# Latent columns ahead of the banded attention's in the input projection, normalising after the values, and another order at the start of the feed-forward stage

## The chip, the cores and the metric

The kernel runs on one core of a Trainium2 chip. The time is device microseconds of one launch: the median of three runs was 1651.15 us before the change (1648.31 to 1651.73). A profile was taken of one more execution. The engines are TensorE (PE in the rows, PEld its weight loads), VectorE (DVE), ScalarE (ACT), GpSimd (POOL) and SyncE (SP, which here only starts transfers). Each takes its instructions in a fixed order and waits at the first whose inputs or places are not ready.

## What is computed

One layer of a hybrid model, for a prompt of 128 tokens and a latent grid of 1024. Each is modulated, goes through one input projection, then through three kinds of heads, an output projection and a gated feed-forward part:

```
z = h @ w_in                       # 1024 -> 256 + 128 + 32 | 256 + 128 + 128 | 512
o_mla = softmax(q k^T) v           # latent attention, 8 heads, 1024 + 256 keys
o_swa = softmax(band, context, sink) v     # banded attention, 4 heads
cu = conv_module(u)                # 31 taps over 256 channels
x = x + g1 * (concat(o_mla, o_swa, cu) @ w_out)
x = x + g2 * ((silu(dwconv(h @ w_up)[gate]) * dwconv(h @ w_up)[value]) @ w_down)
```

The first 416 columns of `z` (cq, ckv, kr) belong to the latent attention, the next 512 to the banded one, the last 512 to the convolution.

## The kernel before

There are nine tiles of 128 tokens: tile 0 is the prompt, 1 to 8 the grid. Every float32 product is three matrix products (`mm3`, lines 61 to 63): an operand is split into a rounded high part and the rest, and high by high, high by low and low by high are added up in one bank. So whatever becomes an operand is split first: a copy or cast to the high part on ScalarE, and a subtraction on VectorE (lines 69, 72, 77) or, after a plain copy, two operations on GpSimd (`split_turned`, lines 607 to 609: copy `pf` on ScalarE, `ph` and `pl` on GpSimd).

A scheduler with a model of each engine's times orders the instructions of every engine when the program is built; the order in the source and the tiles' buffers bound it. The stages by the trace:

- To 75 us: loads and modulation. To 126: the convolution's columns (`convolved`). VectorE then works at the taps of the convolution (line 552, 128x1167 each), which fill it until 200 us.
- 126 to 183: the banded attention's 512 columns, for tiles 0 to 4 and then 5 to 8, a tile's product being 24 matmuls. `later_half` calls between them make the modulation's later pieces; their weights are loaded into the places of `cqH` and `cqL`, which are free until the latent columns come. Each tile is rotated on VectorE (lines 434, 439, 440) into `zs`.
- 183 to 232: the latent 416 columns, in three groups of three tiles. Each tile is squared and scaled on ScalarE (lines 529 to 532: `junk`, `zm`), with its root (`rs_b`, line 122) on GpSimd, transposed (line 547) and split into `cqH`, `cqL`, `ckH`, `ckL`. Between the two halves of the last group stands `window_operands`: the transposes (line 475) and splits of `zs` for tiles 1 to 4. Weights of a set of columns are split by `load_w` (lines 307, 308), and the next set takes the places of the last.
- 232 to 375: the banded attention (`Window`), from its scores (line 639) on. Other tasks fill it.
- 405 to 738: the latent attention, 32 `Pair`s of one head and two tiles, each by `PLAN` (line 1006): scores `S` of the next pair, its maxima `M` (lines 958 to 960), exponentials `E` (lines 965, 966), `N` (line 971 adds the two sums, 972 inverts them, 973 multiplies the 128x1280 probabilities `pt`, on GpSimd, in the last pairs on VectorE), and for this pair the turns `T` 0 to 4 (line 980: four transposes; then the split, by GpSimd for the chunks in `POOLC`, else by ScalarE and VectorE) and the products with the values `A` (line 989) into `acc`, a bank with one buffer. `join` (lines 901, 995) adds its two halves into `ot`, and so frees `acc`.
- 740 to 850: the output projection. 850 to 898: the start of the feed-forward part. Its products are made by a scheme of seven products (1 to 7) of sums of quarters. Their right operands `B[n]` are made by `split_b` (lines 1264, 1265) in two halves of the tokens (`e`) from the modulated tiles; the left ones are sums of quarters of the weights, split in `left`. Products 1 and 2 of weight blocks 0 and 1 are made ahead. 898 to 1360: 22 weight blocks `f_`, one after another, in `up`; then the down projection to the end.

Of the kernel before, what the change touches and what calls it, by code (L numbers as in the profile page):

```python
# [51 lines left out]
def step_kernel(ctx, tc, i, o):  # L52
# [229 lines left out]
    zs = zsp.tile([P, NT, 512], F32, name="zs")  # L282
# [77 lines left out]
    wide = [lat.tile([P, 2, TOK], F32, name=n) for n in ("cqH", "cqL")]  # L360
# [7 lines left out]
    wide = itertools.cycle([t[:, n, 0:D].rearrange("p (k n) -> p k n", k=2) for t in wide for n in range(2)] + [None, None])  # L368
# [51 lines left out]

    for t in range(NT):
        if t in (0, 5):
            prods = in_products(range(t, 5 if t == 0 else NT), 512, lambda: later_half(*halves.pop(0), in_products.last))
        ps = prods[t]
        if t == 0:
            act.copy(zs[:, t, :], ps)
            sp.dma_start(out=o["s_k"].rearrange("a b p h d -> p (a b h d)"), in_=zs[:, 0, 256:384])
            sp.dma_start(out=o["s_v"].rearrange("a b p h d -> p (a b h d)"), in_=zs[:, 0, 384:512])
        else:
            act.copy(zs[:, t, 384:512], ps[:, 384:512])  # L430
            tab = zp.tile([P, 2, 64], F32, name="ropes", bufs=4)
            sp.dma_start(out=tab, in_=i["rope_s"][(t - 1) * P:t * P])
            t2 = zp.tile([P, 384], F32, name="rot", bufs=1)
            dve.tensor_mul(zs[:, t, 0:384].rearrange("p (h d) -> p h d", h=6), ps[:, 0:384].rearrange("p (h d) -> p h d", h=6),
                           tab[:, 0:1, :].broadcast_to([P, 6, 64]))
            xs, b = (x.rearrange("p (h e s q) -> p h e s q", h=6, e=2, s=2) for x in (ps[:, 0:384], t2))
            sn = tab[:, 1, :].rearrange("p (e s q) -> p e s q", e=2, s=2)
            for s in range(2):
                dve.tensor_mul(b[:, :, :, s, :], xs[:, :, :, 1 - s, :], sn[:, :, s, :].unsqueeze(1).broadcast_to([P, 6, 2, 16]))
            dve.tensor_add(zs[:, t, 0:384], zs[:, t, 0:384], t2)  # L440

    later_half(*halves.pop(0), in_products.last)
    cqH, cqL = (lat.tile([P, 2, TOK], F32R, name=n) for n in ("cqH", "cqL"))

    kvg = zp.tile([P, P], F32, name="kvg", bufs=1)
    sp.dma_start(out=kvg, in_=i["kvg"].broadcast_to([P, P]))
    sp.dma_start(out=zkr[:, NT:, :], in_=i["kr_c"].rearrange("(t p) d -> p t d", p=P))
    ckc = zp.tile([P, 384], F32, name="zm", bufs=4)[:, 0:256].rearrange("p (t d) -> p t d", t=2)
    sp.dma_start(out=ckc, in_=i["ckv_c"].rearrange("(t p) d -> p t d", p=P))
    tp = wtile()  # L450
    for t in range(2):
        pe.transpose(tp[:, t * P:(t + 1) * P], ckc[:, t, :], ident)
    split(ckH[:, TOK:], ckL[:, TOK:], tp[:, :256])

    ws = [load_w(w_in[:, 2 * j:2 * j + 2, 0:416], 2, 416, pool) for j in range(4)]
# [134 lines left out]
    put_v(0, NT, zs[:, :, 384:512])  # L590
    late = [lambda g0=g0, g1=g1, j=j: put_task(g0, g1, j) for g0, g1 in ((5, 9), (0, 1)) for j in (2, 0, 1)]
# [350 lines left out]
    class Pair:  # L942
# [48 lines left out]
        def join(self):  # L991
# [3 lines left out]
            dve.tensor_add(ot[j][r:r + 64, a:b], self.acc[0:64, :], tmp)  # L995
# [8 lines left out]
    POOLC = (1,3,4)  # L1004
# [237 lines left out]


    second = {}
    for h, n in enumerate((1, 2)):
        raw = part(F32)
        sp.dma_start(out=raw, in_=i["w_up"][1, :, h * 512:(h + 1) * 512])
        second[n] = part(), part()
        split_w(*second[n], raw)
    ahead_t = mq.tile([P, PLACE], F32, name="q0")  # L1250
    ahead = [ahead_t[:, n * H:(n + 1) * H] for n in range(2)]
    ps = Banks()
    for n, to in zip((1, 2), ahead):
        for e in range(2):
            product(ps[n][:, e * 512:(e + 1) * 512], second[n], n, e)
        act.copy(halved(to), halved(ps[n]))


    def split_b(n, stacks, src, los):
        B[n] = [by_k(place(stack, name)) for stack, name in stacks]  # L1260
        hi, lo = B[n]
        for e in range(2):
            cs = slice(e * HN, (e + 1) * HN)
            act.copy(hi[:, :, cs], src[:, :, cs])  # L1264
            los[e].tensor_sub(lo[:, :, cs], src[:, :, cs], f(hi[:, :, cs]))  # L1265
# [16 lines left out]
    def left(f_):  # L1282
# [17 lines left out]
        for n, src in ((1, a11), (6, s2), (2, a12), (7, s3), (5, s1), (4, a22), (3, s4)):  # L1300
            if f_ > 1 or n not in first:
# [5 lines left out]
    def up(f_):  # L1307

        ops = left(f_)
        ps = Banks()  # L1310

        for es in ((0,), (1,)) if f_ == 0 else ((0, 1),):
# [199 lines left out]
```

## Time and profile before

| | us |
|---|---|
| Median of three runs | 1651.15 |
| The profiled execution | 1651.77 |
| Its span in the profile | 1650.0 |
| TensorE busy | 1535.8 (93%) |
| VectorE busy | 1025.8 (62%) |
| GpSimd busy | 913.1 (55%) |
| ScalarE busy | 735.8 (45%) |

The times in the rows are from the start of the span; 1.77 us of the profiled execution lie around it. A row of TensorE's time gives a matmul's length with its pipeline, so consecutive starts tell the step; the granted clock is the share of full speed (2.4 GHz) that the throttle granted, and 0.5 is 1.2 GHz.

### The profile page before, as it was taken

The numbers are of one execution on the slowest core, as the hardware profiler recorded it, in microseconds if no ns is written. First come the engines' busy times: TensorE is split into PE (matmuls) and PEld (weight loads), VectorE is DVE, ScalarE is ACT, GpSimd is POOL, SyncE is SP. The second block draws the span as 40 slices with busy tenths as digits, with TensorE's granted clock in tenths as the row PEclk, the third lists the DMA queues.
The fourth block names the chain that finished last, engine by engine and source line by source line (L and its number), as shares of the span: only waits on it lengthen the run. The fifth ranks groups of instructions, "written<-read, shape, count | busy, mean of one in ns | idle before, by whom it ended". The sixth has DMA issues, their size and how long they took to land.

```text
span 1650.0 us, 24931 instructions
## 1 busy us (share of the span) xinstructions
PE 1535.8 (93%) x9278; PEld 1360.3 (82%) x9278; DVE 1025.8 (62%) x1508; ACT 735.8 (45%) x1449; POOL 913.1 (55%) x938
## 2 busy tenths in 40 slices
PE   6899987878999898889998999999999999999997
PEld 3777776766888777778888999999999998878885
DVE  1689847856776777682268776767766776132322
ACT  3510265675677766662244443343443344232331
POOL 1511457962888786762426977777777753130221
PEclk8899988987999999999998999999999999999999
DMA  9463111341010103035531222222222246343341
GB/s 345 156 218 130 62 34 48 100 121 21 8 34 11 30 15 93 26 120 169 175 107 62 67 80 81 80 68 62 72 81 81 80 150 217 112 161 108 114 150 51
DMA packets 86831, 160.88 MB, mean 98 GB/s; under 512 B 8831, under 2 KB 49063, under 8 KB 86711
## 3 DMA queue, kind: packets, MB, share of 16 engines
q1 hardware_dynamic: 72135, 137.34, 25.6%
q0 software_dynamic: 3552, 12.52, 2.9%
q10 hardware_dynamic: 11024, 9.44, 1.7%
q8 instruction: 73, 1.20, 0.3%
q14 instruction: 47, 0.39, 0.1%
HBM read 124.09 MB, written 34.46 MB: 96 GB/s over the span
## 4 chain that ended last, share of the span: by engine, by line
PE 60%; DVE 7%; ACT 4%; issue 3%; POOL 1%; DMA 0%; ACTq 0%; POOLq 0%; DVEq 0%
PE u L63 15%; PE u L62 15%; PE u L61 14%; PE acc L989 3%; PE po L61 2%; PE po L62 2%; PE po L63 2%; PE w L980 2%; ACT pt L965 1%; PE s L61 1%; PE s L62 1%; DVE mst L958 1%; PE s L63 1%; DVE mst L971 1%; DVE mst L960 1%
## 5 line engine op out<-in xcount | busy, mean ns | idle before, releaser
L1304 POOL TENSOR_TENSOR as<-q,as 128x512 fp32r<-128x512 f32 x100 | 171.6, 1735 | 109.1 <-ACT as L1303 109.1
L1303 ACT CAST as<-q 128x512 fp32r<-128x512 f32 x145 | 88.7, 619 | 200.7 <-PE u L62 183.1
L1337 DVE SCALAR_TENSOR_TENSOR h<-h,fw,h 128x1154 f32<-128x1154 f32 x88 | 156.1, 1775 | 25.7 <-ACT h L1335 23.3
L609 POOL TENSOR_TENSOR pl<-pf,ph 128x512 fp32r<-128x512 f32 x106 | 136.4, 1291 | 3.0
L1376 DVE TENSOR_TENSOR as<-as 128x384 fp32r<-128x384 f32 (+2 forms) x62 | 39.7, 641 | 128.7 <-ACT as L1375 76.2
L980 PE MATMUL w<-ident,pt 128*128 128x128 f32 x640 | 98.7, 281 | 21.5 <-DVE pl L69 14.6
L980 PEld LDWEIGHTS w<-ident,pt 128*128 128x128 f32 x640 | 75.0, 143 | 34.0 <-DVE pl L69 18.9
L973 POOL TENSOR_SCALAR pt<-pt,mst 128x1280 f32<-128x1280 f32 x60 | 80.1, 1335 | 40.2 <-DVE mst L972 37.1
L552 DVE SCALAR_TENSOR_TENSOR y<-u,cw,y 128x1167 f32<-128x1167 f32 x60 | 94.0, 1584 | 0.6
L608 POOL TENSOR_SCALAR ph<-pf 128x512 fp32r<-128x512 f32 x106 | 67.1, 636 | 48.4 <-ACT pf L607 42.5
L1375 ACT CAST as<-as 128x384 fp32r<-128x384 f32 (+2 forms) x62 | 32.9, 533 | 124.6 <-DMA as<-y_d 115.8
L1368 POOL TENSOR_TENSOR as<-q,as 128x512 fp32r<-128x512 f32 x18 | 23.0, 1291 | 117.1 <-ACT as L1367 90.8
L958 DVE TENSOR_REDUCE mst<-s 128x1 f32<-128x1024 f32 x64 | 77.3, 1215 | 12.6 <-PE s L63 12.4
L965 ACT ACTIVATE pt<-s,mst 128x1024 f32<-128x1024 f32 x64 | 71.8, 1121 | 29.5 <-DVE mst L960 26.5
L62 PE MATMUL u<-h,as 128*128 128x290 f32 (+1 forms) x248 | 80.8, 326 | 0.5 <-DVE h L1265 0.5
L61 PE MATMUL u<-h,as 128*128 128x290 f32 (+1 forms) x248 | 80.9, 326 | 0.2 <-ACT h L1264 0.2
L63 PE MATMUL u<-h,as 128*128 128x290 f32 (+1 forms) x248 | 80.4, 324 | 0.0
L308 POOL TENSOR_TENSOR wl<-raw,wh 128x1024 fp32r<-128x1024 f32 (+1 forms) x8 | 25.9, 3241 | 94.4 <-ACT wh L307 66.1
L607 ACT COPY pf<-w 128x512 f32<-128x512 f32 x106 | 62.1, 590 | 27.8 <-PE w L980 13.9
L69 DVE TENSOR_TENSOR pl<-w,ph 128x512 fp32r<-128x512 f32 (+1 forms) x104 | 65.8, 638 | 10.9 <-ACT ph L68 10.2
L1335 ACT ACTIVATE h<-h,vec,fw 128x1154 f32<-128x1154 f32 x44 | 59.6, 1354 | 25.2 <-DVE h L1329 14.7
L68 ACT CAST ph<-w 128x512 fp32r<-128x512 f32 (+1 forms) x104 | 56.7, 551 | 26.5 <-PE w L980 9.4
(555 smaller groups left out, 5603.0 us busy)
## 6 DMA issues: line engine op xcount, KB each, us to landing
q<-in_w_up SPq DMA_DIRECT2D x44, 512.0 KB, 3.6
q<-in_w_down SPq DMA_DIRECT2D x34, 512.0 KB, 3.7
y_d<-h SPq DMA_DIRECT2D x22, 577.0 KB, 5.5
q<-ot_d POOLq DMA_DIRECT2D x18, 512.0 KB, 5.8
as<-y_d SPq DMA_DIRECT2D x44, 192.0 KB, 3.3
adaw<-in_ada_w SPq DMA_DIRECT2D x8, 1024.0 KB, 8.0
cqH<-in_ada_w SPq DMA_DIRECT2D x12, 512.0 KB, 4.7
adaw<-in_ada_w SPq DMA_DIRECT2D x10, 512.0 KB, 8.5
```

Of the source, the lines that this page charges most:

```text
L61: pe.matmul(out, lh, rh, start=first, stop=False)
L62: pe.matmul(out, lh, rl, start=False, stop=False)
L63: return pe.matmul(out, ll, rh, start=False, stop=last)
L552: dve.scalar_tensor_tensor(y[q], u[q][:, j:j + CONVN], cw[:, q, j:j + 1], y[q], ALU.mult, ALU.add)
L609: pool.tensor_sub(pl[:, :n], pf[:, :n], f(ph[:, :n]))
L958: dve.tensor_reduce(st[:, 0:1], self.s1[d], op=ALU.max, axis=AX.X, negate=True)
L965: act.activation(pt[:, 0:1024], self.s1[d], AF.Exp, bias=st[:, 2:3], accum_out=st[:, 3:4])
L973: eng.tensor_scalar(pt, pt, st[:, 6:7], 1.0, ALU.mult, ALU.mult)
L980: pe.transpose(tp[:, (2 * d + e) * P:(2 * d + e + 1) * P], self.pt[e][:, (2 * c + d) * P:(2 * c + d + 1) * P], ident)
L1303: act.copy(ops[n][0], src)
L1304: (dve if f_ == 0 or n in (1, 4) else pool).tensor_sub(ops[n][1], src, f(ops[n][0]))
L1337: dve.scalar_tensor_tensor(y[:, m], z[:, m, j:j + YW], fw[:, j, v:v + 1], y[:, m], ALU.mult, ALU.add)
```

## The change

Three parts. **The projection**: the latent columns come first and the banded attention's after them, in groups of three tiles; the modulation's weights go into the place that `zs` takes later, and the `later_half` calls stand between the halves of the latent groups; `window_operands` stands ahead of the last group of the banded columns; the values of tiles 5 to 8 and 0 (`put_v`) are made in late tasks of the banded attention. **The latent attention**: line 973 is gone. The reciprocal is turned along the columns by two transposes of a 128x64 broadcast (`along`, line 602 of the changed kernel) into the upper half of `acc`'s bank, and `join` multiplies the sum by it (lines 999, 1000). Chunk 2's split goes from VectorE to GpSimd. **The feed-forward start**: products 1 and 2 of weight block 2 are made ahead too (48 matmuls), the operands' splits go by halves of the tokens around them, and product 4 comes ahead of 5 in every block.

```diff
-    zs = zsp.tile([P, NT, 512], F32, name="zs")
+    wide = zsp.tile([P, NT, 512], F32, name="zs")
...
-    wide = [lat.tile([P, 2, TOK], F32, name=n) for n in ("cqH", "cqL")]
+    cqH, cqL = (lat.tile([P, 2, TOK], F32R, name=n) for n in ("cqH", "cqL"))
...
-    wide = itertools.cycle([t[:, n, 0:D].rearrange("p (k n) -> p k n", k=2) for t in wide for n in range(2)] + [None, None])
+    wide = itertools.cycle([wide[:, 2 * n:2 * n + 2, :] for n in range(4)] + [None, None])
...
-            ws += [load_w(w_in[:, 2 * j:2 * j + 2, 416:928], 2, 512, pool) for j in range(len(ws), len(ws) + 2)]
+            ws += [load_w(w_in[:, 2 * j:2 * j + 2, 0:416], 2, 416, pool) for j in range(len(ws), len(ws) + 2)]
...
-    for t in range(NT):
-        if t in (0, 5):
-            prods = in_products(range(t, 5 if t == 0 else NT), 512, lambda: later_half(*halves.pop(0), in_products.last))
-        ps = prods[t]
...
-    ws = [load_w(w_in[:, 2 * j:2 * j + 2, 0:416], 2, 416, pool) for j in range(4)]
...
     for g0, g1 in groups:
...
-        zm, prods = {}, in_products(range(g0, g1), 416, window_operands if g1 == NT else None)
+        zm, prods = {}, in_products(range(g0, g1), 416, lambda: later_half(*halves.pop(0), in_products.last))
...
+    ws = [load_w(w_in[:, 2 * j:2 * j + 2, 416:928], 2, 512, pool) for j in range(4)]
+    zs = zsp.tile([P, NT, 512], F32, name="zs")
+    for g0, g1 in groups:
+        if g1 == NT:
+            window_operands()
+        prods = in_products(range(g0, g1), 512)
+        for t in range(g0, g1):
+            ps = prods[t]
...
+                dve.tensor_add(zs[:, t, 0:384], zs[:, t, 0:384], t2)
...
-    put_v(0, NT, zs[:, :, 384:512])
-    late = [lambda g0=g0, g1=g1, j=j: put_task(g0, g1, j) for g0, g1 in ((5, 9), (0, 1)) for j in (2, 0, 1)]
+    put_v(1, 5, zs[:, 1:5, 384:512])
+    late = [lambda g0=g0, g1=g1, j=j: (put_task(g0, g1, j), put_v(g0, g1, zs[:, g0:g1, 384:512]) if j == 2 else None)
+            for g0, g1 in ((5, 9), (0, 1)) for j in (2, 0, 1)]
...
+    def along(out, inv):
+
+        pe.transpose(out, inv.broadcast_to([P, 64]), ident)
...
         def norm(self, d):
-            st, pt = self.st[d], self.pt[d]
-            eng = dve if self.last else pool
+            st = self.st[d]
             dve.tensor_add(st[:, 5:6], st[:, 3:4], st[:, 4:5])
             dve.reciprocal(st[:, 6:7], st[:, 5:6])
-            eng.tensor_scalar(pt, pt, st[:, 6:7], 1.0, ALU.mult, ALU.mult)
...
             if c == 0:
-                self.acc = pacc.tile([P, 256], F32, name="acc")
+                both = pacc.tile([P, 512], F32, name="acc")
+                self.acc, self.inv = both[:, 0:256], both[0:64, 256:512]
+                for d in range(2):
+                    along(self.inv[:, d * P:(d + 1) * P], self.st[d][:, 6:7])
...
             tmp = joined(self.acc, 256)
-            dve.tensor_add(ot[j][r:r + 64, a:b], self.acc[0:64, :], tmp)
+            dve.tensor_add(tmp, self.acc[0:64, :], tmp)
+            dve.tensor_mul(ot[j][r:r + 64, a:b], self.inv, tmp)
...
-    POOLC = (1,3,4)
+    POOLC = (1,2,3,4)
...
+    def products_ahead(f_):
+
+        ahead[f_] = [ahead_t[:, (2 * f_ - 2 + n) * H:(2 * f_ - 1 + n) * H] for n in range(2)]
+        ops, ps = {}, Banks()
+        for h, n in enumerate((1, 2)):
+            raw = part(F32)
+            sp.dma_start(out=raw, in_=i["w_up"][f_, :, h * 512:(h + 1) * 512])
+            ops[n] = part(), part()
+            split_w(*ops[n], raw)
+        for n, to in zip((1, 2), ahead[f_]):
+            for e in range(2):
+                product(ps[n][:, e * 512:(e + 1) * 512], ops[n], n, e)
+            act.copy(halved(to), halved(ps[n]))
+
+    products_ahead(1)
...
-    split_b(6, ((tsp, "b6h"), (tsp, "b6l")), t2, (dve, dve))
-    split_b(7, ((tsp, "b7h"), (tsp, "b7l")), t3, (dve, dve))
-    split_b(3, ((tsp, "b3h"), (tsp, "b3l")), b22, (dve, dve))
...
+    def operands_b(e):
+        cs = slice(e * HN, (e + 1) * HN)
+        split_b(6, t2, e, ((tsp, "b6h"), (tsp, "b6l")))
+        split_b(7, t3, e, ((tsp, "b7h"), (tsp, "b7l")))
+        split_b(3, b22, e, ((tsp, "b3h"), (tsp, "b3l")))
+        dve.tensor_sub(b22[:, :, cs], b22[:, :, cs], t2[:, :, cs])
+        if e == 0:
+            split_b(4, t4, e, ((tsp, "b4h"), (tsp, "b4l")))
+
+    operands_b(0)
+    products_ahead(2)
+    operands_b(1)
...
-        for n, src in ((1, a11), (6, s2), (2, a12), (7, s3), (5, s1), (4, a22), (3, s4)):
-            if f_ > 1 or n not in first:
+        for n, src in ((1, a11), (6, s2), (2, a12), (7, s3), (4, a22), (5, s1), (3, s4)):
+            if f_ > 2 or n not in first:
...
+            dve.tensor_add(g1, prod(4), at(u3))
             p5 = prod(5)
             dve.tensor_add(g2, p5, at(u3))
             dve.tensor_add(at(u2), p5, at(u2))
-            dve.tensor_add(g1, prod(4), at(u3))
             dve.tensor_add(v2, prod(3), at(u2))
```

Three places in the engines' orders. First TensorE at the end of the projection, before (`g` is a product's bank, `zm` a scaled latent tile, `s` a score):

```order
L61 MATMUL g<-wh,hHb 128x416
L62 MATMUL g<-wl,hHb 128x416
L63 MATMUL g<-wh,hLb 128x416
L547 MATMUL w<-ident,zm 128x128 x6
L639 MATMUL s<-hLa,hHa 128x256
L640 MATMUL s<-hLa,hHa 128x256
```

and changed, and with it VectorE there (`rot` and `zs` are a tile's rotation, `vst` the values, `sink` a logit written into the score's bank):

```order
L61 MATMUL g<-wh,hHb 128x512
L62 MATMUL g<-wl,hHb 128x512
L63 MATMUL g<-wh,hLb 128x512
L642 MATMUL s<-hLa,hHa 128x256 x2
L643 MATMUL s<-hLa,hHa 128x256
L645 MATMUL s<-hLa,hHa 128x256
```

```order
L540 TENSOR_TENSOR zs<-g,ropes 128x384
L545 TENSOR_TENSOR rot<-g,ropes 128x12x16 x2
L546 TENSOR_TENSOR zs<-zs,rot 128x384
L540 TENSOR_TENSOR zs<-g,ropes 128x384
L545 TENSOR_TENSOR rot<-g,ropes 128x12x16 x2
L579 TENSOR_TENSOR vst<-zs,vst 128x8x64
L579 TENSOR_TENSOR vst<-zs,vst 128x2x64
L546 TENSOR_TENSOR zs<-zs,rot 128x384
L639 COPY s<-sink 128x1 x2
```

The six transposes of scaled tiles ahead of the first score are gone; the last rotation and a copy of the sink stand on VectorE ahead of it.

Second, TensorE between two pairs of the latent attention, before and changed (`acc` is the bank, `mst` holds the reciprocal):

```order
L61 MATMUL w<-kT_3869,q_3908 128x256
L62 MATMUL w<-kT_3870,q_3908 128x256
L63 MATMUL w<-kT_3869,q_3908 128x256
L980 MATMUL w<-ident,pt 128x128 x4
L989 MATMUL acc<-ph,vtb 128x256
```

```order
L61 MATMUL w<-kT_3868,q_5832 128x256
L62 MATMUL w<-kT_3869,q_5832 128x256
L63 MATMUL w<-kT_3868,q_5832 128x256
L602 MATMUL acc<-ident,mst 64x128 x2
L993 MATMUL acc<-ph,vtb 128x256
```

and VectorE where a pair is joined, before and changed:

```order
L69 TENSOR_TENSOR pl<-w,ph 128x512
L995 TENSOR_TENSOR ot<-acc,join 64x256
L958 TENSOR_REDUCE mst<-s_5546 128x1
L938 TENSOR_TENSOR ot<-w,join 64x128 x2
L69 TENSOR_TENSOR vtb<-w,vtb 128x4x64
```

```order
L961 TENSOR_REDUCE mst<-s_5580 128x1
L999 TENSOR_TENSOR join<-acc,join 64x256
L941 TENSOR_TENSOR ot<-w,join 64x128 x2
L1000 TENSOR_TENSOR ot<-acc,join 64x256
L69 TENSOR_TENSOR vtb<-w,vtb 128x4x64
```

Two transposes into `acc` stand ahead of a pair's first product with the values, and the bank is free one VectorE operation later.

Third, the start of the feed-forward stage: TensorE behind the product 2 of block 1 (`b1` to `b7` are right operands, `as` left ones), before and changed:

```order
L63 MATMUL u<-b2h,as 128x290
L61 MATMUL u<-b6h,as 128x290
L61 MATMUL u<-b7h,as 128x290
L62 MATMUL u<-b7l,as 128x290
L63 MATMUL u<-b7h,as 128x290
L61 MATMUL u<-b7h,as 128x290
```

```order
L63 MATMUL u<-b2h,as 128x290
L61 MATMUL u<-b1h,as 128x290
L62 MATMUL u<-b1l,as 128x290
L63 MATMUL u<-b1h,as 128x290
L61 MATMUL u<-b1h,as 128x290
L62 MATMUL u<-b1l,as 128x290
```

and VectorE, the operands' splits, before and changed:

```order
L1265 TENSOR_TENSOR b3l<-h_8266,b3h 128x4x290
L1265 TENSOR_TENSOR b6l<-h_8263,b6h 128x4x290
L1265 TENSOR_TENSOR b7l<-h_8264,b7h 128x4x290
L1273 TENSOR_TENSOR h_8266<-h_8266,h_8263 128x4x290
L1265 TENSOR_TENSOR b4l<-h_8265,b4h 128x4x290
L1265 TENSOR_TENSOR b6l<-h_8263,b6h 128x4x290
L1273 TENSOR_TENSOR h_8266<-h_8266,h_8263 128x4x290
L1265 TENSOR_TENSOR b4l<-h_8265,b4h 128x4x290
```

```order
L1277 TENSOR_TENSOR b6l<-h_8358,b6h 128x4x290
L1322 TENSOR_TENSOR as<-q_8370,as 128x512
L1277 TENSOR_TENSOR b7l<-h_8359,b7h 128x4x290
L1277 TENSOR_TENSOR b4l<-h_8360,b4h 128x4x290
L1322 TENSOR_TENSOR as<-q_8370,as 128x512
L1277 TENSOR_TENSOR b3l<-h_8361,b3h 128x4x290
L1277 TENSOR_TENSOR b6l<-h_8358,b6h 128x4x290
L1277 TENSOR_TENSOR b4l<-h_8360,b4h 128x4x290
L1284 TENSOR_TENSOR h_8361<-h_8361,h_8358 128x4x290
```

48 matmuls with `b1` and `b2` stand where the first with `b6` stood, and splits of left operands (line 1322) stand between those of right ones.

## Rows read from the trace of the kernel before

**Rows 1.** Four stretches: us, then busy us per engine (instructions), granted clock, DMA share, GB/s.
```profile
183.00:232.00 49.00, 49.00 (x276) 44.93 (x274) 24.97 (x36) 21.62 (x73) 25.17 (x56) 1.00 0.07 20
405.00:748.00 343.00, 306.92 (x1996) 267.90 (x1995) 248.26 (x484) 235.80 (x532) 268.75 (x280) 0.98 0.15 45
850.00:902.00 52.00, 45.29 (x290) 42.97 (x289) 46.46 (x61) 30.59 (x43) 24.96 (x13) 0.87 0.16 56
902.00:1360.00 458.00, 458.00 (x3418) 458.00 (x3417) 331.12 (x290) 177.52 (x227) 330.21 (x264) 1.00 0.26 82
```

**Rows 2.** TensorE in order of time: start, length, line, tile [idle before, its releaser].
```profile
234.24 0.44 PE L547 MATMUL w<-ident,zm 128*128 128x128 f32 x2 [2.02 <-ACT zm L532]
239.50 0.69 PE L547 MATMUL w<-ident,zm 128*128 128x128 f32 x2 [4.82 <-ACT zm L532]
239.83 0.56 PE L639 MATMUL s<-hLa,hHa 128*128 128x256 f32 x1
```

**Rows 3.** VectorE in order of time, 183 to 197 us.
```profile
183.36 0.54 DVE L434 TENSOR_TENSOR zs<-g,ropes 128x384 f32<-128x384 f32 x1
183.82 0.60 DVE L439 TENSOR_TENSOR rot<-g,ropes 128x192 f32<-128x192 f32 x2
...
186.16 2.22 DVE L440 TENSOR_TENSOR zs<-zs,rot 128x384 f32<-128x384 f32 x1
...
196.40 0.55 DVE L440 TENSOR_TENSOR zs<-zs,rot 128x384 f32<-128x384 f32 x1
```

**Rows 4.** The page's costliest groups: the rest of an input weight, on GpSimd.
```profile
L308 POOL TENSOR_TENSOR wl<-raw,wh 128x1024 fp32r<-128x1024 f32 (+1 forms) x8 | 25.9, 3241 | 94.4 <-ACT wh L307 66.1
```

**Rows 5.** Groups by line, 405 to 748: count, busy us, mean ns, idle before.
```profile
L609 POOL TENSOR_TENSOR pl<-pf,ph 128x512 fp32r<-128x512 f32 x90 | 115.9, 1293 | 2.4
L980 PE MATMUL w<-ident,pt 128*128 128x128 f32 x638 | 97.9, 281 | 21.5 <-DVE pl L69 14.6 <-DVE q L72 2.4 <-ACT pf L607 1.7
L973 POOL TENSOR_SCALAR pt<-pt,mst 128x1280 f32<-128x1280 f32 x58 | 77.4, 1335 | 15.3 <-DVE mst L972 12.1 <-DVE mst L960 2.1 <-ACT pf L607 0.6
...
L608 POOL TENSOR_SCALAR ph<-pf 128x512 fp32r<-128x512 f32 x90 | 56.5, 631 | 35.4 <-ACT pf L607 34.1 <-PE acc L989 0.8
...
L69 DVE TENSOR_TENSOR pl<-w,ph 128x512 fp32r<-128x512 f32 x70 | 47.7, 685 | 6.0 <-ACT ph L68 5.5
...
L971 DVE TENSOR_TENSOR mst<-mst 128x1 f32<-128x1 f32 x61 | 30.1, 493 | 7.1 <-ACT pt L966 6.9
```

**Rows 6.** Chain of waits that ended last, 405 to 748, shares by line.
```profile
by line: PE acc L989 12.5%; PE w L980 9.8%; issue 7.3%; ACT pt L965 7.2%; PE s L61 5.4%; PE s L62 5.0%; PE s L63 4.8%; DVE mst L958 4.7%; DVE mst L971 4.3%; DVE mst L960 3.4%; PE w L61 3.1%; DVE pl L69 2.9%; PE w L63 2.6%; ACT pt L966 2.6%;
```

**Rows 7.** Waits, 405 to 748: engine, line, waited for; us in total, times, longest.
```profile
PE w L980 <- DVE pl L69: 14.6, 16, 3.2
...
PE s L61 <- ACT pt L965: 5.5, 10, 1.0
...
PE acc L989 <- POOL pl L609: 3.2, 5, 1.4
...
PE acc L989 <- DVE ot L995: 2.3, 3, 1.8
```

**Rows 8.** VectorE in order of time, 712 to 718 us.
```profile
712.32 0.42 DVE L995 TENSOR_TENSOR ot<-acc,join 64x256 f32<-64x256 f32 x1
...
716.85 1.26 DVE L971 TENSOR_TENSOR mst<-mst 128x1 f32<-128x1 f32 x1
718.03 0.15 DVE L960 TENSOR_TENSOR mst<-mst 128x1 f32<-128x1 f32 x1
```

**Rows 9.** GpSimd at the same place.
```profile
716.81 1.28 POOL L609 TENSOR_TENSOR pl<-pf,ph 128x512 fp32r<-128x512 f32 x1
```

**Rows 10.** TensorE at the start of the feed-forward stage.
```profile
864.57 0.40 PE L61 MATMUL u<-b2h,as 128*128 128x290 f32 x1 [2.00 <-ACT h L1155]
...
872.23 0.58 PE L62 MATMUL u<-b6l,as 128*128 128x290 f32 x1 [1.36 <-DVE b6l L1265]
...
877.34 0.61 PE L62 MATMUL u<-b6l,as 128*128 128x290 f32 x1 [1.37 <-DVE b6l L1265]
```

More of the change, by code (lines that the diff above doesn't have):

```diff
@@ L419, in in_products @@
         return ps
-    for t in range(NT):
-        if t in (0, 5):
-            prods = in_products(range(t, 5 if t == 0 else NT), 512, lambda: later_half(*halves.pop(0), in_products.last))
-        ps = prods[t]
[L425 to L453, printed above, removed]
-    ws = [load_w(w_in[:, 2 * j:2 * j + 2, 0:416], 2, 416, pool) for j in range(4)]
     def copy_half(to, src, g, sl):
@@ L519, in step_kernel @@
     sp.dma_start(out=sink, in_=i["sink"].broadcast_to([P, 4]))
+    kvg = zp.tile([P, P], F32, name="kvg", bufs=1)
+    sp.dma_start(out=kvg, in_=i["kvg"].broadcast_to([P, P]))
+    sp.dma_start(out=zkr[:, NT:, :], in_=i["kr_c"].rearrange("(t p) d -> p t d", p=P))
+    ckc = zp.tile([P, 384], F32, name="zm", bufs=4)[:, 0:256].rearrange("p (t d) -> p t d", t=2)
+    sp.dma_start(out=ckc, in_=i["ckv_c"].rearrange("(t p) d -> p t d", p=P))
+    tp = wtile()
+    for t in range(2):
+        pe.transpose(tp[:, t * P:(t + 1) * P], ckc[:, t, :], ident)
+    split(ckH[:, TOK:], ckL[:, TOK:], tp[:, :256])
     for g0, g1 in groups:
         n = (g1 - g0) * P
-        zm, prods = {}, in_products(range(g0, g1), 416, window_operands if g1 == NT else None)
+        zm, prods = {}, in_products(range(g0, g1), 416, lambda: later_half(*halves.pop(0), in_products.last))
         for t in range(g0, g1):
@@ L1241, in halved @@
         return x.rearrange("p (e n) -> p e n", e=2)[:, es[0]:es[-1] + 1, 0:HN]
[L1244 to L1249, printed above, removed]
-    ahead_t = mq.tile([P, PLACE], F32, name="q0")
[L1251 to L1256, printed above, removed]
@@ L1259, in split_b @@
[L1259 to L1265, printed above, removed]
-    (t2, t3), (t4, b22) = hf32
-    split_b(6, ((tsp, "b6h"), (tsp, "b6l")), t2, (dve, dve))
-    split_b(7, ((tsp, "b7h"), (tsp, "b7l")), t3, (dve, dve))
-    split_b(3, ((tsp, "b3h"), (tsp, "b3l")), b22, (dve, dve))
+    ahead_t = mq.tile([P, PLACE], F32, name="q0")
@@ new lines, in step_kernel @@
+    ahead = {}
+    def products_ahead(f_):
[10 more added lines that the diff above has]
+            act.copy(halved(to), halved(ps[n]))
@@ new lines, in step_kernel, with split_b @@
+    products_ahead(1)
+    ahead[0] = p1, p2
+    (t2, t3), (t4, b22) = hf32
+    def split_b(n, src, e, stacks):
+        if e == 0:
+            B[n] = [by_k(place(stack, name)) for stack, name in stacks]
+        hi, lo = (x[:, :, e * HN:(e + 1) * HN] for x in B[n])
+        x = src[:, :, e * HN:(e + 1) * HN]
+        act.copy(hi, x)
+        dve.tensor_sub(lo, x, f(hi))
+    def operands_b(e):
[4 more added lines that the diff above has]
+        dve.tensor_sub(b22[:, :, cs], b22[:, :, cs], t2[:, :, cs])
+        if e == 0:
+            split_b(4, t4, e, ((tsp, "b4h"), (tsp, "b4l")))
@@ L1292, in left @@
             load_up(f_)
-            if f_ == 2:
+            if f_ == 3:
                 sums_t = mq.tile([P, PLACE], F32, name="q0")
-            s1, s2, s3, s4 = (part(F32) if f_ == 1 else sums_t[:, n * 512:(n + 1) * 512] for n in range(4))
+            s1, s2, s3, s4 = (part(F32) if f_ < 3 else sums_t[:, n * 512:(n + 1) * 512] for n in range(4))
             pool.tensor_add(s1, a21, a22)
@@ L1319, in up @@
             (v1, v2), (g1, g2) = [[at(z[:, m, 1 + th * H:1 + (th + 1) * H]) for th in range(2)] for m in range(2)]
-            q1, q2 = ((p1, p2), ahead)[f_] if f_ < 2 else (p1, None)
-            if f_ > 1:
+            q1, q2 = ahead[f_] if f_ in ahead else (p1, None)
+            if f_ not in ahead:
                 act.copy(at(q1), prod(1))
```

23 lines of the change are left out of this document (18 added, 5 removed).

## The prediction

> **What bounds the kernel now.** I read the stretches first, then the seams between stages in order of time, and inside the latent attention the waits, the groups by line and the chain. The stretches [rows 1] show two kinds of stage. From 902 to 1360 TensorE is busy for all of 458.00 us, and so it is from 183 to 232: there only fewer matmuls help. From 405 to 748 it is busy for 306.92 of 343, and from 850 to 902 for 45.29 of 52 at a granted clock of 0.87: there order and waits count. The third place with room is the seam at 232, where TensorE stands still for most of 7.6 us [rows 2]. The change touches just these three places. Its sum is made against the profiled execution, 1651.8 us, which lies 0.6 above the median of the runs.
>
> **The projection.** The last product ends at 234.24 - 2.02 = 232.2, and the first score starts at 239.83 [rows 2]. Between them TensorE transposes six scaled latent tiles and waits 2.02 and 4.82 us for their scaling on ScalarE. In the changed order the latent tiles are followed by products of the banded columns, so these waits have cover. What is late next is the rotation of the last banded tile on VectorE, 0.54 + 0.60 + 0.55 = 1.7 us [rows 3], with the values' splits and a copy of the sink ahead of the first score: some three small operations, each between the 0.15 of a tiny one [rows 8] and 0.6, 0.5 to 1.8 together. I take 3 us for all of it. Gain 7.6 - 3 = 4.6, taken as 4.5; if all goes under cover, 7.6.
>
> What is moved can cost. The rotations of eight tiles, 8 x 1.7 = 13.5 us, go behind the taps, into the time in which VectorE was busy for 24.97 of 49 us [rows 1]; that covers them. Beside GpSimd's work one addition of a rotation took 2.22 instead of 0.55 [rows 3]; should all three tiles of the last group meet that, the last is late by up to 3 us. The weights of the banded columns now come second. Their last two pieces, each 3.24 us on GpSimd [rows 4], must be ready when the first group's first half is through: 36 matmuls of 512 columns, by the 458.00 / 3418 = 0.134 us of one with 290 columns [rows 1] about 0.236 each, 8.5 us. Two pieces take 6.5 and a cast ahead. That fits barely; the same exchange stands in the trace before, at the start of 183 to 232, and TensorE lost nothing there [rows 1]. I take nothing, and one piece, 3.2 us, as the bound. The loads for the modulation stay as many and as large, on SyncE's queue, and their place is free earlier: nothing. The late values are a subtraction and a copy in a stage in which no engine is full: nothing, bounds 1 us either way. Sum for this part: **-4.5 us**, from -8 to +3.
>
> **The latent attention.** TensorE idles for 343 - 306.92 = 36.1 us [rows 1]. Five terms.
>
> (a) The probabilities no longer pass through the sum, the reciprocal and the multiplication on their way to the turns. On the chain line 971 has 4.3% of 343, 14.7 us; line 973 is not in its list, which ends at 2.6%, so it has under 8.9 [rows 6]. That bounds the gain at 24 and at 0 below. The four waits in rows 7 explain 14.6 + 5.5 + 3.2 + 2.3 = 25.6 of the 36.1 idle, by other causes; 10.5 are left for this one and small ones. I take -9.
>
> (b) Chunk 2's rest goes from VectorE (685 ns) to GpSimd (631 + 1293) [rows 5]; ScalarE copies in either case. TensorE waited 14.6 for VectorE's rests, of two chunks, and 3.2 for GpSimd's, of three [rows 7]. Half of the first goes, a third of the second comes: -7.3 + 1.1, about -6. GpSimd doesn't become the bound: in each of 28 pairs it loses 2 x 1.335 and gains 1.924, -21 of its 268.75.
>
> (c) `along`: 64 transposes more. One transpose costs 97.9 / 638 = 0.153 us [rows 5], so 9.8; a tenth of the stage is idle and hides its share. +9.
>
> (d) `acc` is free one VectorE operation later, 0.42 us as line 995 [rows 8], or 13.4 for 32 pairs if nothing covers it. TensorE waited for line 995 three times in the stage, 2.3 us [rows 7], and the scheduler has other matmuls to put there. Behind the waiting transposes stand this pair's products and the next scores. +2, between 0 and 13.4.
>
> (e) VectorE's tiny additions wait for GpSimd. Line 971 mostly takes far more than the 0.15 us of an undisturbed one: it started at 716.85, 0.04 after a GpSimd line 609, and took 1.26 to that one's 1.28 [rows 8, 9]. Over the stage this is 61 x (0.493 - 0.15) = 20.9 us for line 971 alone [rows 5]. The long ones lie under lines 608 and 609. These become more by 28 on 90, nearly a third: +6.5 if the whole excess grows with them. But line 971 no longer leads to the turns, only to `along`. +3, between 0 and 6.5.
>
> The Trainium skill says why, on its page SBUF — State Buffer, section Who interferes with whom: a VectorE instruction with two inputs in SBUF contends with a GpSimd instruction that reads SBUF, and whichever comes first holds the shared pair for its whole length. The trace agrees (1.26 under 1.28). By that rule line 973, which reads SBUF as well, counts like the others, and since GpSimd's reading time falls by 21 us here, term (e) would be a gain of about 1 us and the forecast 1634, inside its own range. The trace before can't show it, since line 971 feeds 973 and seldom runs beside it; I keep +3.
>
> Sum: -9 - 6 + 9 + 2 + 3 = **-1 us**. The ends, worked out below as rivals, are far apart.
>
> **The feed-forward start.** From 850 to 902 TensorE idles for 6.7 us, and 45.29 us of work ran at 0.87 of the clock, which is 45.29 x 0.13 = 5.9 us lost; together 12.6 [rows 1]. The first wait, 2.00 for the last tile's modulation, stays. Behind it TensorE waits for VectorE's splits of operand 6, 1.36 and 1.37 the longest [rows 10]; these and the shorter ones are 6.7 - 2.0 = 4.7. The 48 matmuls of block 2, 48 x 0.134 = 6.4 us, are done in this place instead of inside a stage in which TensorE has no gap, so what they fill is gained: up to 4.7, and of the clock's 5.9 what a denser TensorE keeps. I take 4 of these. VectorE is the feeder, busy for 46.46 of 52, and it gets the rests of two more left operands, 0.7 us each by line 69 [rows 5]; if it stays the bound the waits come again behind the 48, and only some 3 us are gained. Blocks 1 and 2 then have five products, 120 x 0.134 = 16.1 us, while VectorE and GpSimd need 331 and 330 us for the stage's 3418 / 168 = 20.3 blocks, 16.3 each [rows 1]: 0 to 2 us are given back, I take 1. Product 4 ahead of 5 moves no work. -4.7 - 4 + 1, about **-8 us**, from -3 to -10.6.
>
> **The rivals.** First, *slower*: the latent attention is bound by TensorE and by `acc`, and the shorter way to the turns brings nothing, since the next wait takes its place. Then (a) is 0 and (b) a small -3, while (c), (d) and (e) cost 9.8 + 13.4 + 6.5: about +26 there, 1651.8 - 4.5 - 8 + 26 = 1665. For it: TensorE is busy for 89% of the stage, and `acc` has one buffer. Against it: 36 us of idle time to fill. It decides from +15.8 there on. Chance 0.14. Second, *the attention gains*: the way to the turns was what spaced the pairs, (a) is worth 20, (b) 7, and (d) is covered: -20 - 7 + 9 = -18, and 1651.8 - 4.5 - 18 - 8 = 1621. For it: lines 971 and 973 stand on the chain. Against it: the chain's greatest shares are TensorE's own [rows 6]. Chance 0.18. Third, *the change doesn't do what it says*: the seam only gets another wait (weights late by 3, rotations late) and the 48 matmuls only put off the waits for VectorE; 0 + 0 - 3, 1649. For it: 2 us of margin at the weights, VectorE at 46.46 of 52. Chance 0.13.
>
> **How the numbers follow.** The forecast: 1651.8 - 4.5 - 1 - 8 = 1638.3, by the median's scale 0.6 less, 1638. Its chance is 0.55, with 1631 to 1645 as its own range. About 0.2%, 3.3 us, is what a measurement can tell from no change. Faster: 0.55 + 0.18, and a little of the third, 0.74; same: the most of the third, 0.12; slower: the first, 0.14. The range 1621 to 1653 takes in the third and most of the second, and leaves the first out.
>
> **What would show it.** Right: the first score at about 235 by the clock of the trace before, with no wait for scaled latent tiles ahead; from the first score to the output projection about as long as before, with fewer waits for VectorE's `pl` and new ones at `along`; block 0 of the feed-forward part at its end within some 4 us of gain although 48 more matmuls stand ahead, and block 2 at 16 us. Wrong: waits at the first banded products for `wl`; TensorE waiting at `along` for line 1000 in most pairs; a longer stretch of lowered clock in the feed-forward start; a wait in blocks 1 and 2 longer than 2 us.

## The result, and the profile after

The changed kernel takes 1661.47 us (median of six runs, 1659.97 to 1664.5), the kernel before 1650.52 on the same chips: a ratio of 1.0074, with a 95% interval of 1.0061 to 1.0088. It is 11 us slower by the medians, 12 by the ratio. Forecast were 1638, and a range up to 1653; the time lies above it.

The profiled execution of the changed kernel has a span of 1659.2 us, 9.2 more than before. Where they come from is read at marks that both traces have:

| mark | before | after | moved by |
|---|---|---|---|
| last product of the input projection starts | 231.65 | 252.56 | +20.9 |
| first score of the banded attention | 239.83 | 256.06 | +16.2 |
| its last score with the context | 342.5 | 359.3 | +16.8 |
| first product with the values, latent attention | 407.5 | 422.0 | +14.5 |
| the last one | 743.4 | 757.2 | +13.8 |
| last transpose of the modulation ahead of the feed-forward part | 859.1 | 872.9 | +13.8 |
| end of the span | 1650.0 | 1659.2 | +9.2 |

So 20.9 us are lost inside the input projection, 4.7 are won at its end, and all that lies behind wins some 7 more. TensorE's stretches after, which answer to [rows 1] (us, then busy us per engine with instructions, granted clock, DMA share, GB/s):

```profile
126.00:183.00 57.00, 45.38 (x235) 36.82 (x231) 43.48 (x37) 13.23 (x50) 30.91 (x38) 0.90 0.31 106
183.00:232.00 49.00, 45.62 (x204) 34.42 (x204) 29.45 (x30) 13.48 (x36) 26.80 (x34) 0.94 0.15 43
...
902.00:1360.00 458.00, 456.47 (x3399) 456.00 (x3398) 361.72 (x295) 176.55 (x231) 342.80 (x269) 1.00 0.25 79
```

From 126 to 232 TensorE, which had no gap there before, idles for 11.6 + 3.4 = 15 us, and the clock falls to 0.90 and 0.94. What it waits for, from 75 to 260 (engine, line, waited for; us in total, times, longest):

```profile
PE w L520 <- ACT zm L505: 13.8, 3, 8.7
PE s L642 <- DVE s L639: 3.1, 1, 3.1
PE s L643 <- POOL hLa L422: 1.2, 1, 1.2
PE g L62 <- POOL wl L308: 1.1, 1, 1.1
```

Three waits, 13.8 us, stand at the transposes of the scaled latent tiles (line 520; 547 before). The scaling on ScalarE waits for the tile's root, which is made by two tiny operations on GpSimd, lines 119 and 122. The longest of these waits in TensorE's order of time, 8.67 us (the others are 2.83 and 2.33), and the seam at the end of the projection:

```profile
157.11 0.48 PE L520 MATMUL w<-ident,zm 128*128 128x128 f32 x1 [8.67 <-ACT zm L505]
...
252.56 0.39 PE L63 MATMUL g<-wh,hLb 128*128 128x512 f32 x1
256.06 0.48 PE L642 MATMUL s<-hLa,hHa 128*128 128x256 f32 x2 [3.11 <-DVE s L639]
```

GpSimd over the same time, and below it VectorE:

```profile
139.77 4.34 POOL L119 TENSOR_SCALAR rs_a<-ms 128x2 f32<-128x2 f32 x1 [12.11 <-ACT junk L503]
144.20 0.71 POOL L122 TENSOR_TENSOR rs_b<-rs_a,expo 128x2 f32<-128x2 f32 x1
...
147.47 9.08 POOL L122 TENSOR_TENSOR rs_b<-rs_a,expo 128x2 f32<-128x2 f32 x1
...
158.93 0.70 POOL L122 TENSOR_TENSOR rs_b<-rs_a,expo 128x2 f32<-128x2 f32 x1
```

```profile
137.26 6.79 DVE L550 SCALAR_TENSOR_TENSOR y<-u,cw,y 128x1167 f32<-128x1167 f32 x5
...
147.85 8.14 DVE L550 SCALAR_TENSOR_TENSOR y<-u,cw,y 128x1167 f32<-128x1167 f32 x6
```

An operation on 128x2 elements that takes 0.70 us took 9.08. It began at 147.47, VectorE's six taps of the convolution ran back to back from 147.85 to 155.99, and it ended at 156.55, 0.56 behind the last of them. The first `rs_a` did the same: it began at 139.77, inside the second of five taps, and ended at 144.11, the taps at 144.05. In the kernel before, the first root began at 197.67, and the last of these taps ended at 200.68; the change puts the roots under the taps.

### The profile page after: what moved, and what is told of

Its sections match the earlier page's. It is cut to its first block, busy times and chain, and to the rows that moved or that the text cites. A ratio compares the mean times of both kernels' runs of the same rounds, so it can differ in the third digit from the quotient of the medians.

```text
span 1659.2 us, 25080 instructions
## 1 busy us (share of the span) xinstructions
PE 1540.6 (93%) x9342; PEld 1367.2 (82%) x9342; DVE 1040.3 (63%) x1509; ACT 732.1 (44%) x1452; POOL 915.2 (55%) x937
## 4 chain that ended last, share of the span: by engine, by line
PE 68%; DVE 8%; issue 4%; ACT 4%; POOL 4%; DMA 1%; POOLq 0%; DVEq 0%; ACTq 0%; SPq 0%
PE u L62 14%; PE u L63 14%; PE u L61 14%; PE acc L993 3%; PE w L981 3%; PE po L61 2%; PE po L62 2%; PE po L63 2%; PE s L61 2%; PE s L63 2%; PE s L62 2%; PE w L61 1%; PE w L62 1%; PE w L63 1%; ACT pt L968 1%
## 5 line engine op out<-in xcount | busy, mean ns | idle before, releaser
L1355 DVE SCALAR_TENSOR_TENSOR h<-h,fw,h 128x1154 f32<-128x1154 f32 x88 | 186.3, 2124 | 32.8 <-ACT h L1353 30.3
L612 POOL TENSOR_TENSOR pl<-pf,ph 128x512 fp32r<-128x512 f32 x136 | 175.4, 1294 | 7.0
L1321 ACT CAST as<-q 128x512 fp32r<-128x512 f32 x139 | 83.9, 616 | 174.7 <-PE u L62 149.7
L611 POOL TENSOR_SCALAR ph<-pf 128x512 fp32r<-128x512 f32 x136 | 85.2, 630 | 109.0 <-ACT pf L610 102.9
L981 PE MATMUL w<-ident,pt 128*128 128x128 f32 x640 | 97.7, 283 | 16.2 <-DVE pl L69 8.1
L981 PEld LDWEIGHTS w<-ident,pt 128*128 128x128 f32 x640 | 76.5, 145 | 26.3 <-DVE pl L69 11.6
L610 ACT COPY pf<-w 128x512 f32<-128x512 f32 x136 | 78.5, 590 | 26.6 <-PE w L981 12.7
L61 PE MATMUL s<-kT,q 96*128 96x512 f32 x128 | 55.5, 438 | 9.4 <-ACT pt L968 9.3
L62 PE MATMUL u<-b6l,as 128*128 128x290 f32 (+1 forms) x194 | 59.5, 307 | 1.9 <-DVE b6l L1277 1.9
L61 PE MATMUL u<-b4h,as 128*128 128x290 f32 (+1 forms) x194 | 59.4, 306 | 0.7 <-ACT b4h L1276 0.7
L61 PE MATMUL u<-b6h,as 128*128 128x290 f32 (+1 forms) x194 | 59.4, 306 | 0.6 <-ACT b6h L1276 0.6
```

What stands on the lines that cost most here:

```text
L61: pe.matmul(out, lh, rh, start=first, stop=False)
L62: pe.matmul(out, lh, rl, start=False, stop=False)
L610: act.copy(pf[:, :n], tp[:, :n])
L611: pool.tensor_scalar(ph[:, :n], pf[:, :n], 1.0, 0.0, ALU.mult, ALU.add)
L612: pool.tensor_sub(pl[:, :n], pf[:, :n], f(ph[:, :n]))
L981: pe.transpose(tp[:, (2 * d + e) * P:(2 * d + e + 1) * P], self.pt[e][:, (2 * c + d) * P:(2 * c + d + 1) * P], ident)
```

## The experiments

### Each part alone

The three parts of the diff, each applied to the kernel before without the others, and the second and third together.

> The kernel before with the projection part of the change alone. Theory: the whole loss lies here, since between the two traces the first score of the banded attention moved by +16.3 us and nothing behind it added; the tiny operations on GpSimd that make the roots of the latent tiles (lines 119 and 122) wait for VectorE's taps. Expected: 14 to 18 us slower than before, TensorE waiting some 14 us at the transposes of scaled latent tiles. Rival, the parts hinder each other or the loss comes with the latent attention: within 4 us of before.

Measured: 1.0111 (1.0082 to 1.0140), +17 to +18 us. TensorE's wait is the same 13.8 us, 3 times, longest 8.7. The part is the loss, all of it.

> The kernel before with late normalising alone (reciprocal turned by transposes, chunk 2 on GpSimd). Theory: the two traces put it at -1 us from the first to the last product with the values; expected between -4 and +2 us. Rival, the first one of the prediction (transposes on TensorE, the bank free later, more waits of VectorE for GpSimd): +10 to +25 us.

Measured: 0.9955 (0.9939 to 0.9971), -7.4 us, more than the traces had promised. The first rival of the prediction, +10 to +25, falls.

> The kernel before with the new order of the feed-forward start alone. Theory: the two traces put it at -6.3 us up to the end of weight block 2 and +1.6 given back in block 4; expected -3 to -7 us. Rival, the 48 matmuls only put off the waits for VectorE: within 2 us of before.

Measured: 0.9971 (0.9952 to 0.9990), -4.8 us, as the traces put it.

> The changed kernel with the projection part undone. Theory: the parts add up, so -4 to -9 us against before, some 16 us faster than the changed kernel. Rival, the loss is not in the projection: slower than before as the changed kernel is.

Measured: 0.9917 (0.9887 to 0.9948), 1637.03 us: -13.7, more than the -4 to -9 expected, about the sum of the two as measured alone (-12.2), and faster than either kernel.

### What holds the roots up

Three edits of the changed kernel. The first leaves out all but two of the taps for each half of the channels:

```diff
-        for j in range(1, CW - LT[q]):
+        for j in range(1, 3):
             tap(q, j)
```

> The changed kernel with 2 taps of the convolution for each half of the channels instead of the 31 and 29 of line 556 (the convolution's sum is left out to that extent). VectorE is then nearly idle from 126 to 232 us. Theory, the taps keep GpSimd from its tiny operations: the longest line 122 falls from 9.08 to about 0.7 us, TensorE's wait at the transposes of scaled latent tiles from 13.8 to under 3, and the first score comes at 234 to 240 instead of 256.1 us; 12 to 18 us faster than the changed kernel in the stretch up to it. Rival, the roots are late for another reason (GpSimd's own order, ScalarE): the wait stays above 10 us.

Measured: 0.9950 (0.9928 to 0.9972) against the kernel before. No wait at the transposes is left. Line 122 in the changed kernel and here (count, ns least/median/most, first and last start, form):

```profile
L122 POOL TENSOR_TENSOR rs_b<-rs_a,expo x9: 697/699/9081, 144.2 to 211.6; 128x2 f32<-128x2 f32 x9
```

```profile
L122 POOL TENSOR_TENSOR rs_b<-rs_a,expo x9: 697/702/707, 139.4 to 185.5; 128x2 f32<-128x2 f32 x9
```

The last product starts at 230.76 and the first score at 234.3: the "about 235" that the prediction named as the sign of its being right. That the taps cause the loss is shown; whether by keeping VectorE busy or by what they do in memory is not yet. So the second edit leaves the taps and makes VectorE busier:

```diff
             dve.scalar_tensor_tensor(y[q], u[q][:, j:j + CONVN], cw[:, q, j:j + 1], y[q], ALU.mult, ALU.add)
+            dve.tensor_reduce(gapt, y[q][:, 0:2], op=ALU.max, axis=AX.X)
```

> The changed kernel with a reduction of 2 elements (one input in SBUF) behind each tap on VectorE, 58 of them, some 0.1 us each. Theory, GpSimd's tiny operation only gets its turn where VectorE does something else than a two-input operation between two taps: line 122 takes at most one tap, 1.5 us, the waits at the transposes fall to under 5 us, and the kernel is 8 to 15 us faster than the changed one. Rival, what counts is that VectorE is busy at all, or that a later tap takes its turn first all the same: waits as before, within 3 us of the changed kernel.

Measured: 0.9979 (0.9967 to 0.9991), some 15 us faster than the changed kernel by 60 useless reductions (the expectation says 58; two taps come later). The longest root and the waits lie a little above the 1.5 and 5 us expected. Line 122, the wait, and the stretch from 126 to 232:

```profile
L122 POOL TENSOR_TENSOR rs_b<-rs_a,expo x9: 697/702/1879, 140.0 to 196.4; 128x2 f32<-128x2 f32 x9
```

```profile
PE w L521 <- ACT zm L506: 5.5, 4, 2.1
```

```profile
126.00:232.00 106.00, 99.71 (x502) 79.75 (x500) 91.22 (x126) 31.51 (x97) 50.92 (x75) 1.00 0.24 78
```

VectorE is busy for 91.22 us of these 106, in the changed kernel for 72.93, and yet the longest root is 1.88 us: about one tap and itself. VectorE's load as such is not the cause.

The reduction reads what the tap ahead of it has written, and starts 0.03 us after that tap's end. So it puts two things between two taps: an operation with one input, and a pause. The changed kernel's own later taps tell more. These are six of them, and operations on GpSimd under them; the last row lies under a later row of seven such taps:

```profile
172.10 8.82 DVE L550 SCALAR_TENSOR_TENSOR y<-u,cw,y 128x1167 f32<-128x1167 f32 x6
```

```profile
173.59 0.70 POOL L122 TENSOR_TENSOR rs_b<-rs_a,expo 128x2 f32<-128x2 f32 x1
...
179.60 1.38 POOL L119 TENSOR_SCALAR rs_a<-ms 128x2 f32<-128x2 f32 x1
...
201.66 1.90 POOL L122 TENSOR_TENSOR rs_b<-rs_a,expo 128x2 f32<-128x2 f32 x1
```

Nothing stands between these taps either, and yet GpSimd gets its turn between them and waits for one tap at most. What differs is their spacing. The six taps from 147.85 took 8.14 us, 1.34 from start to start, and each starts 0.07 us before the one ahead of it ends; these six took 8.82, 1.48 from start to start, and each starts 0.03 us after the end of the one ahead. So the root of 9.08 us lies under taps that overlap; with a pause between them, the tiny operation is late by one tap. The trace of the projection part alone has the same two long ones, 4.35 and 9.08 us; a run that changes the spacing alone is not here. Such single taps make TensorE's two shorter waits, 2.83 and 2.33 us. Why the earlier taps overlap, the rows don't show; two halves of the channels in turn, each with a sum of its own, would allow it.

The third edit takes the roots off GpSimd:

```diff
-            r = rstd_of(ms, 2)
+            dve.tensor_scalar(ra, ms, 1.0, EPS, ALU.mult, ALU.add)
+            act.activation(rq, ra, AF.Sqrt)
+            dve.reciprocal(r, rq)
```

> The changed kernel with the latent tiles' roots off GpSimd: sum and reciprocal are tiny operations on VectorE between the taps, the square root is on ScalarE (one more table load, about 1.3 us). Theory: a tiny operation waits for one tap at most, 1.4 us, the waits at the transposes fall from 13.8 to 1 to 4 us; 10 to 18 us faster than the changed kernel, so 1642 to 1651. Rival, the order of TensorE's transposes among the products is at fault, whatever engine makes the root: waits stay above 10 us.

Measured: 0.9963 (0.9948 to 0.9979), 1644.48 us, 17 less than the changed kernel; the wait at the transposes is gone altogether. TensorE's only wait from 126 to 232 is now:

```profile
PE g L62 <- POOL wl L308: 0.9, 1, 0.9
```

The order of the transposes, the rival, is not at fault.

The same edit on the projection part alone:

> The projection part alone, with the latent tiles' roots off GpSimd. The same part with the roots on GpSimd is +17 us. Theory, the wait of those roots for the taps is all of its loss, and its gain at the seam is then seen: between -5 and +2 us against before, the first score between 234 and 240 us. Rival, swapping the columns costs for other reasons too: above +6.

Measured: 1.0003 (0.9989 to 1.0016). The wait of the roots is the whole loss of the part. The first score stands at 237.26, 2.6 us earlier than before, and that is all that the exchange of the columns is worth with the roots out of the way:

```profile
237.26 0.48 PE L643 MATMUL s<-hLa,hHa 128*128 128x256 f32 x2 [3.11 <-DVE s L640]
238.91 0.58 PE L644 MATMUL s<-hLa,hHa 128*128 128x256 f32 x1 [1.17 <-POOL hLa L422]
```

### The terms of the latent attention

Late normalising won 7.4 us, but is it the way to the turns or the chunk? The second part of the change with one number put back:

```diff
-    POOLC = (1,2,3,4)
+    POOLC = (1,3,4)
```

> The kernel before with late normalising, but chunk 2's split left on VectorE. Late normalising with chunk 2 on GpSimd gave -7.4 us. By the prediction's terms the chunk is worth -6 and all the rest of the part -1 with its added waits for GpSimd (+3) in it: expected -1 to +2 here. Rival, the way to the turns is the gain and the chunk none: -5 to -9 as with it.

Measured: 0.9920 (0.9897 to 0.9942), -13.2 us. Both expectations miss: without the chunk's move the part wins more. So the chunk's move alone, on the kernel before:

```diff
-    POOLC = (1,3,4)
+    POOLC = (1,2,3,4)
```

> The kernel before with chunk 2's split moved from VectorE to GpSimd and nothing else; line 973 stays on GpSimd, so that engine gets 1.92 us more for each of 28 pairs. The prediction's term (b): -6 us. By the two runs of late normalising, with and without the chunk (0.9955 and 0.9920), it costs some 6 us there; theory: it costs 5 to 15 us here, where GpSimd is fuller, since tiny additions on VectorE wait for GpSimd's operations and GpSimd's queue gets longer.

Measured: 1.0207 (1.0181 to 1.0233), +34 us, more than twice what was expected. TensorE waits longer for GpSimd's rests, and for the exponentials and the join too, against the 5.5, 3.2 and 2.3 us of [rows 7]:

```profile
PE s L61 <- ACT pt L965: 18.1, 28, 1.6
PE acc L989 <- POOL pl L609: 8.6, 17, 0.9
PE acc L989 <- DVE ot L995: 7.8, 11, 1.9
```

GpSimd is busy for 326.26 of 370.70 us there; that it sets the pace is likely, not shown. The latent attention from the first product with the values to the last, in the kernel before, the changed one, late normalising, late normalising without the chunk, and the chunk alone:

```profile
407.50:743.40 335.90, 299.82 (x1961) 262.05 (x1960) 245.01 (x478) 231.97 (x523) 266.72 (x274) 0.97 0.14 42
```

```profile
422.00:757.20 335.20, 304.22 (x2031) 270.53 (x2030) 230.15 (x478) 232.62 (x527) 249.11 (x276) 0.97 0.15 45
```

```profile
401.70:731.40 329.70, 303.01 (x2030) 268.03 (x2029) 232.36 (x478) 233.46 (x527) 250.04 (x276) 0.98 0.14 42
```

```profile
401.50:726.30 324.80, 298.98 (x2030) 263.69 (x2029) 232.60 (x508) 231.39 (x527) 194.11 (x216) 0.99 0.14 43
```

```profile
408.30:779.00 370.70, 318.34 (x1961) 271.40 (x1960) 232.75 (x448) 233.45 (x523) 326.26 (x334) 0.95 0.13 39
```

GpSimd's busy time (the fifth number) falls from 266.72 to 194.11 where the chunk stays, and the stage is shortest there.

### Put together

> The kernel before with late normalising (chunk 2 left on VectorE) and the new feed-forward start; the projection as before. If the parts add up: 0.992 and -5 us, so 1629 to 1634 us, -17 to -22 against before. Rival, the scheduler's order for the two together takes back some of it: above 1636.

Measured: 0.9892 (0.9873 to 0.9911), 1634.83 us: -17.8, as the parts add up.

> All three parts with the latent tiles' roots off GpSimd (as in the run with the root on ScalarE, 0.9963) and chunk 2 left on VectorE. Theory, chunk 2 on GpSimd costs 6 to 9 us here too: 1635 to 1640. Rival, behind the swapped projection late normalising gains nothing whatever chunk 2 does: 1642 to 1647.

Measured: 0.9888 (0.9866 to 0.9909), 1633.33 us: -18.5, a little more than expected. Against the run with the root on ScalarE, which differs by the chunk alone, that is 12 us: late normalising does gain behind the swapped projection, once the chunk stays on VectorE. These last two kernels are the fastest here, and level with one another: the exchange of the columns adds nothing that can be measured.

## Why the prediction was wrong

**The projection, -4.5 forecast, +16 measured: the step that failed is "what is moved can cost".** It counted the rotations, the weights, the modulation's loads and the values, and left out that the latent tiles' own work, two operations on GpSimd for each tile, moves with the columns from behind the taps to under them. The prediction itself had told that VectorE's two-input operations and GpSimd's hold each other up, and priced it for VectorE's rotations (+3) and for its tiny additions. It never asked the same in the other direction, though [rows 3] and the taps' 100 us were at hand. The seam was right: from the start of the last product to the first score it was 8.2 us before and 3.5 after, 4.7 won for 4.5 forecast, by the rotation and the sink's copy as named. The weights cost 1.1 us for 0 forecast and 3.2 as the bound. Of the 20.9 lost, 14.9 are the waits (13.8 + 1.1); the clock can make the rest, by an estimate of 91.00 us of work from 126 to 232 at 0.92, about 7. Had it asked, a wait of one tap for each tiny operation would have been the natural price. The run with the reductions shows about what that costs, 5.5 us of waits and a kernel still 3.5 us faster than before; the loss comes with the whole rows of overlapping taps.

**The latent attention, -1 forecast, -0.7 measured in the changed kernel: a right sum of wrong terms.**

- (a), the way to the turns, and (c), `along`: without the chunk the stage is 11.1 us shorter, where (a) and (c) together were forecast at 0. TensorE's busy time did not rise by 9 but stayed (299.82 and 298.98, the clock at 0.97 and 0.99) with 64 transposes more, and its idle time fell from 36.1 to 25.8. By an estimate from the granted clocks (299.82 x 0.97 and 298.98 x 0.99), its work grew by about 5 us at full clock, which the higher clock gave back (two digits of the clock leave some 2 us either way); of the 9.8 forecast for the transposes no more can be seen.
- (b), chunk 2, has the wrong sign. Forecast were -6; with late normalising it costs 6 us (0.9955 and 0.9920), behind the swapped projection 12, and without late normalising 34. The step that failed is that TensorE's shorter wait for VectorE's rests was counted as won. Late normalising with the chunk on GpSimd, and without:

```profile
PE w L982 <- DVE q L72: 8.1, 6, 1.7
...
PE w L982 <- DVE pl L69: 5.9, 8, 3.1
```

```profile
PE w L982 <- DVE pl L69: 14.8, 19, 3.5
...
PE w L982 <- DVE q L72: 0.4, 1, 0.4
```

More than half of the wait for `pl` went, as forecast, and the waits for GpSimd's rests did not grow (3.0 us with the chunk, 3.8 without). But other waits took its place: for `q`, a query's split in line 72, and for the exponentials (6.4 and 2.7). TensorE's idle time stayed level, 26.7 and 25.8 us, and its work took 4.0 us longer, at a granted clock of 0.98 and 0.99. Where line 973 stays, GpSimd is busy for 88% of the time and the chunk costs most. By which way GpSimd's load comes to cost this is not shown.

- (d): TensorE waited at `along` for line 1000 for 0.7 us in all, for +2 forecast.
- (e): lines 971 and 960, 51.6 us together before, fell to 44.6 in the changed kernel and to 32.6 without the chunk's move, where +3 was forecast:

```profile
L963 DVE TENSOR_TENSOR mst<-mst 128x1 f32<-128x1 f32 x60 | 23.8, 396 | 1.0
L973 DVE TENSOR_TENSOR mst<-mst 128x1 f32<-128x1 f32 x61 | 20.8, 342 | 12.5 <-ACT pt L969 12.4
```

```profile
L964 DVE TENSOR_TENSOR mst<-mst 128x1 f32<-128x1 f32 x60 | 18.6, 310 | 0.9
L974 DVE TENSOR_TENSOR mst<-mst 128x1 f32<-128x1 f32 x61 | 14.0, 230 | 6.7 <-ACT pt L970 6.6
```

The prediction set the rule of the Trainium skill's page SBUF — State Buffer (section Who interferes with whom) against this term: any GpSimd instruction that reads SBUF counts, the old line 973 too. These rows agree with the rule's sign, not with the forecast's. But in the trace before, none of the additions longer than 0.25 us lies under line 973 (they lie under lines 608, 609 and, twice, 1001), so that line 973 counts is not shown, and why the long ones became fewer stays open.

**The feed-forward start, -8 forecast, -4.6 in the traces and -4.8 alone: a term of the right kind, too large.** In the same 52 us (850 to 902 before [rows 1], 864 to 916 now) TensorE does 46 matmuls more, 6.2 us by 0.134 each; of these 1.9 come from less idle time, and the rest, 4.3, from the clock, which stayed at 1.00 (4 forecast). The mis-sized step is that the 48 matmuls fill the waits behind VectorE's splits, 4.7 us. From 864 to 916 TensorE still idles for 4.8, of which 2.1 behind VectorE's rests and 2.5 behind ScalarE's high parts; what is gone is the first wait, 2.00, which the prediction said would stay:

```profile
864.00:916.00 52.00, 47.17 (x336) 44.71 (x335) 46.74 (x61) 30.37 (x46) 23.16 (x16) 1.00 0.21 66
```

1.3 us are given back in block 4 at one wait for VectorE, two blocks later than named.

**The rivals.** The changed kernel came out as slow as the first rival's price (1665 for 1661), by another mechanism and in another place; that its time is near is no merit. The third named the right stage with the wrong cause.

**What stays open.** With chunk 2 on GpSimd, late normalising shortens the stage by 6 us alone and by 0.7 behind the swapped projection. Pair by pair the traces run level to the start of the 28th; the next three pairs take 34.0 us in the changed kernel and 26.9 where the projection is undone. The engines' orders differ there, since the scheduler draws them anew for each program, and one `along` waited 2.4 us behind two of the next pair's maxima. Whether that order is the whole of it wasn't tried.

## What to carry to other kernels

When a step is moved, list every engine on which its small work runs, and look at what VectorE does beside GpSimd in the new place: a 0.7 us operation on GpSimd took as long as a whole row of two-input operations on VectorE where these overlapped, and one of them longer where they did not. Ask of each engine that is "only" 78% busy what one operation more per step does before moving work onto it; a wait of TensorE for it is no measure of its room. A sum that comes out right says little on its terms: measure each part alone before the next is built on it.

## What the runs showed of the hardware

GpSimd doesn't get in between two taps that overlap. The Trainium skill's page SBUF — State Buffer, section Who interferes with whom, says that whichever engine issues first gets the shared pair for the whole instruction and the other fully blocks; one would expect a wait of one tap, 1.4 us. The later taps of the changed kernel agree with that: each starts 0.03 us after the one ahead of it has ended, and line 119 took 1.38 us there. The earlier ones do not: each starts 0.07 us before the one ahead of it has ended, and line 122 waited through six of them, 9.08 us, line 119 through the end of one and three more, 4.34. With a 2-element reduction between the taps the longest was 1.88.

And TensorE paid twice for such waits: 15 us of idle time from 126 to 232 came with a granted clock of 0.92. The kernel with the reductions, which idled for 6.3 us there, and the kernels without the wait had 1.00.
